# A bidirectional RWKV-7 scan: half of the output norm two slots later, three copies and squares reordered, and the old state added by one whole-array product

## The chip, the cores and the metric

The kernel runs on one core of one Trainium2 chip, as one launch. TensorE (PE, with its weight loads as PEld), VectorE (DVE), ScalarE (ACT), GpSimd (POOL) and SyncE (SP, which here only issues DMAs) each work through their own instruction queue in order. The metric is the device time of one execution in microseconds (us), lower is better. Before the change the median of three runs is 4229.61 us (4223.09 to 4233.41).

## The reference

The kernel computes two encoder layers over 1280 tokens (256 of a prompt, 1024 of a sample) with 1024 channels: a bidirectional RWKV-7 mixer with an MLP, then a neighbourhood attention with an MLP. The change lies in the mixer alone. Cut to that:

```python
def step(S, inp):                       # one token; S is 64 x 64 for each of 16 heads
    r_t, w_t, k_t, v_t, a_t, b_t = inp
    sa = jnp.einsum('bhvk,bhk->bhv', S, a_t)
    S = S * w_t[:, :, None, :] + sa[..., None] * b_t[:, :, None, :] + v_t[..., None] * k_t[:, :, None, :]
    return S, jnp.einsum('bhvk,bhk->bhv', S, r_t)
# run forward (d = 0) and backward (d = 1); y is the sum of both
mu = jnp.mean(y, axis=-1, keepdims=True)
var = jnp.mean(jnp.square(y - mu), axis=-1, keepdims=True)
y = ((y - mu) * lax.rsqrt(var + GN_EPS)).reshape(B, T, C) * lnx_g + lnx_b
y = y + (bonus * vf).reshape(B, T, C)
out = (y.astype(h.dtype) * g) @ w_o
```

## The kernel before

**Jobs and slots.** The recurrence is taken in chunks of 64 tokens. Two heads share the 128 partitions, one in the lower and one in the upper 64. A job is 16 chunks of such pairs; there are ten jobs (two of prompt chunks, eight of sample chunks), and each takes 16 steps, one a slot. In step i the forward direction works on chunk i and the backward one on chunk 15 - i, so that step 15 finishes the last of the job's y. A state starts anew at slot 0 of jobs 2 to 9 and at slots 0, 4, 8 and 12 of jobs 0 and 1.

**The order.** All work of the scan is registered with `at(slot, function)`. The list is sorted by slot time, and each of PE, DVE, ACT and POOL gets its instructions in just that order; no planner moves them. SP's DMAs are issued in the order of the same list. A job's preparation (masks, a triangular inverse by rank-1 updates on DVE, lines 874 to 880, and its transfers) is registered up to 41 slots ahead of the job itself, so that in every slot the engines also do work for later jobs.

**One step** (`scan_step`, k is the step's number over all jobs). It uses two PSUM banks, bx and by, of two each, taken in turn by k: A and sn (the new state) lie in bx, Y and U in by.
- s0 at i - 0.64: PE adds the products of v into sn (`bx<-vv,ll`), Y (`by<-vv,zz`) and A (`bx<-vv,zz`).
- s1 at i: PE adds the old state's products into Y and A (`by<-S,x`, `bx<-S,x`).
- s1c at i + 0.1: ACT copies A to up (line 1040).
- s2 at i + 0.3: PE makes U from up (`by<-up,qq`).
- s2b at i + 0.32: PE adds the old state into sn, by products with the identity (`bx<-S,cst`). It is left out where a state starts or ends.
- s0 of step i + 1 follows at i + 0.36.
- s2c at i + 0.38: ACT copies U to u (line 1060).
- s3 at i + 0.58: PE adds u's products into sn and Y (`bx<-u,ll`, `by<-u,zz`).
- s3c at i + 0.66: ACT scales sn to the new state S (line 1075), in two instructions.
- s4 at i + 0.75: ACT copies Y to y (line 1080), or in steps 8 to 15 to y2 (line 1083), which s5 at i + 0.97 adds to y on DVE (line 1087).

Products of 64x64 name a quadrant of the PE array by the partitions that they read and write. Those of s2, s2b and `bx<-u,ll` read and write the same half (diagonal quadrants); `bx<-vv,ll` and `bx<-vv,zz` read one half and write the other (off-diagonal). Each 32-bit float product is issued as two passes.

**Beside the steps**, for later steps, PE makes kps (line 960, one PSUM buffer), which DVE masks to zz (line 965) at .95 of each slot and ACT copies to ll (line 970) at .74. The products kps of the next slot can't start until both have read it.

**The norm of a job's y** (`scan_post`) is made in two halves of eight chunks: the first takes the middle chunks 4 to 11, the second chunks 0 to 3 and 12 to 15. Each half is a chain registered from t0 on: bonus times v on DVE (p0) and a bias on POOL, mean (p1) and subtraction (p2) on DVE, squares on ACT (p2b, line 1138), their sum on DVE (p2c, line 1142), rsqrt on DVE and ACT (p3, with Ln and Exp, lines 1151 and 1152), scaling on DVE (p4) and POOL, eight transposing products on PE (tr, line 1167, zps), and p5, a copy to zt on ACT (line 1171) with eight DMAs to z_d that POOL issues (line 1176). The squares' tile and zt share one buffer:

```python
st["sq"] = self.yp.tile([P, 8, 64], F32, name="ysq", tag="ysq", bufs=1)
zt = self.yp.tile([P, 4, 2, 64], F32, name="zt", tag="ysq", bufs=1)
```

t0 is 12.9 for the first half and 16.9 for the second, which so falls into slots 1 to 5 of the next job; the second half of the last job has times of its own.

Of the kernel before, what the change touches and what calls it, by code (L numbers as in the profile page):

```python
# [24 lines left out]
HALVES = ((slice(0, 64), slice(64, 128)), (slice(64, 128), slice(0, 64)))  # L25
# [24 lines left out]
class Trunk:  # L50
# [739 lines left out]
    def at(self, t, f, level=3):  # L790
        self.todo.append((t, len(self.todo), f, level))
# [204 lines left out]
    def scan_step(self, at, J, st, grp, k, i, new, end):  # L996
        nc = self.nc
        mm = lambda out, a, b, start, stop: nc.tensor.matmul(out, a, b, start=start, stop=stop, skip_group_check=True)  # L998
        second = i >= 8
        dirs = []  # L1000
        for d, cc in enumerate((i, 15 - i)):
            m, c0 = grp[cc // 4]
            dirs.append((d, cc // 4, cc % 4, cc, m, c0 + cc % 4))
        pair = lambda t: t[:, :P].rearrange("p (d v) -> p d v", d=2)
        R = {}

        def banks():
            x, y = self.b_x[k % 2], self.b_y[k % 2]
            return pair(x), pair(y), pair(x[:, P:2 * P]), pair(y[:, P:2 * P])
        zz = lambda d, g, c, e: J["zz", d, g, c // 2][:, c % 2, e]  # L1010
        ll = lambda d, g, c, e: J["ll", d, g, c // 2][:, c % 2, e]

        def s0():
            A, Y, sn, U = banks()
            v = J["v"]
            for d, g, c, cc, m, ch in dirs:
                for e, (es, eo) in enumerate(HALVES):
                    if not end:
                        mm(sn[es, d], ll(d, g, c, e)[eo], v[eo, cc], d == 0, False)
            for d, g, c, cc, m, ch in dirs:  # L1020
                yd = 1 - d if second else d
                for e, (es, eo) in enumerate(HALVES):
                    mm(Y[eo, yd], zz(d, g, c, e)[eo, 64:128], v[eo, cc], d == 0, False)
                    mm(A[es, d], zz(d, g, c, e)[eo, 0:64], v[eo, cc], end and d == 0, new)

        def s1():
            A, Y, sn, U = banks()
            R["S"] = S = None if new else st["S"]
            if S is None:
                return  # L1030
            for d, g, c, cc, m, ch in dirs:
                yd = 1 - d if second else d
                for es, eo in HALVES:
                    mm(Y[eo, yd], J["x", d, g][es, 3, c], S[es, d], False, False)
                    mm(A[es, d], J["x", d, g][es, 2, c], S[es, d], False, True)

        def s1c():
            A, Y, sn, U = banks()
            R["up"] = self.sp.tile([P, 2, 64], F32, name="up", tag="up", bufs=2)
            nc.scalar.copy(R["up"], A)  # L1040

        def s2():
            A, Y, sn, U = banks()
            for d, g, c, cc, m, ch in dirs:
                for es, eo in HALVES:
                    mm(U[es, d], J["Q"][es, cc, d], R["up"][es, d], False, True)

        def s2b():
            A, Y, sn, U = banks()
            S = R["S"]  # L1050
            if S is None or end:
                return
            for d in range(2):
                for es, eo in HALVES:
                    mm(sn[es, d], self.ident[es, es], S[es, d], False, False)

        def s2c():
            A, Y, sn, U = banks()
            R["u"] = self.sp.tile([P, 2, 64], F32, name="u", tag="u", bufs=2)
            nc.scalar.copy(R["u"], U)  # L1060

        def s3():
            A, Y, sn, U = banks()
            for d, g, c, cc, m, ch in dirs:
                yd = 1 - d if second else d
                for e, (es, eo) in enumerate(HALVES):
                    if not end:
                        mm(sn[es, d], ll(d, g, c, e)[es], R["u"][es, d], False, True)
                    mm(Y[eo, yd], zz(d, g, c, e)[es, 64:128], R["u"][es, d], False, True)

        def s3c():
            A, Y, sn, U = banks()
            S = st["S"] = self.sp.tile([P, 2, 64], F32, name="S", tag="S", bufs=3)
            for d, g, c, cc, m, ch in dirs:
                nc.scalar.activation(S[:, d], sn[:, d], AF.Copy, scale=self.dall[:, m, d, ch:ch + 1])

        def s4():
            A, Y, sn, U = banks()
            if not second:
                nc.scalar.copy(J["y"][:, i:16 - i:15 - 2 * i], Y)  # L1080
            else:
                R["y2"] = self.sp.tile([P, 2, 64], F32, name="y2", tag="y2", bufs=2)
                nc.scalar.copy(R["y2"], Y)

        def s5():
            y = J["y"][:, 15 - i:i + 1:2 * i - 15]
            nc.vector.tensor_tensor(out=y, in0=R["y2"], in1=y, op=ALU.add)
        at(i - 0.64, s0)
        at(i, s1)
        at(i + 0.1, s1c)  # L1090
        at(i + 0.3, s2)
        at(i + 0.32, s2b)
        at(i + 0.38, s2c)
        at(i + 0.58, s3)
        if not end:
            at(i + 0.66, s3c)
        at(i + 0.75, s4)
        if second:
            at(i + 0.97, s5)

    def scan_post(self, at, J, grp, left):

        nc = self.nc
        for half in range(2):
# [64 lines left out]
            def p5(st=st, runs=runs):  # L1169
                zt = self.yp.tile([P, 4, 2, 64], F32, name="zt", tag="ysq", bufs=1)  # L1170
                nc.scalar.copy(zt, st["zps"])
                for x, (m, c0) in enumerate(runs):
                    dst = self.scr["z_d"][m].rearrange("(e v) (c t) -> e v c t", e=2, t=64)
                    for par in range(2):
                        for e in range(2):
                            nc.gpsimd.dma_start(dst[e, :, c0 + par:c0 + 4:2], zt[64 * par:64 * par + 64, 2 * x:2 * x + 2, e])  # L1176
            t0 = (12.9, 16.9)[half]
            if left == 0 and half == 1:
                when = (-2.0, -1.9, -0.1, 0.0, 0.1, 0.2, 0.3, 0.4, 0.5, 0.6, 0.65, 0.7, 0.9)
            else:  # L1180
                when = (0.2, 0.7, 0.6, 0.95, 1.15, 1.45, 1.6, 1.75, 1.95, 2.3, 3.0, 4.36, 4.62)
            for dt, f in zip(when, (p0, lambda f=lnx: f(1), p1, p2, p2b, p2c, lambda f=p3: f(0), lambda f=p3: f(1), lambda f=p3: f(2), p4,
                                    lambda f=lnx: f(0), tr, p5)):
                at(t0 + dt, f)
# [777 lines left out]
```

## Time and profile before

| | |
|---|---|
| median of three runs | 4229.61 us |
| profiled execution | 4222.5 us |
| its span, first to last instruction | 4220.7 us |
| mean granted TensorE clock | 0.942 |
| scan (first to last copy of up) | 760.5 to 1458.7 us |
| PE, DVE, ACT, POOL busy | 91%, 59%, 36%, 31% of the span |
| copies of up, of u | 160 each, 0.28 and 0.27 us |
| squares (line 1138) | 20, 0.63 us each |

All rows come from one profiled execution. In the timeline a row gives its start, its length, engine, line, operation, the names out<-in, shapes, and in brackets how long the engine had been idle and what ended that. In groups the columns are busy time, mean length in ns of one, and the idle time just before, with what ended it. PE's products are pipelined: a row's end is modelled, its start is what to read.

### The profile page before, as it was taken

What the parts mean: (1) busy time and instruction counts of PE and PEld (TensorE: products, weight loads), DVE (VectorE), ACT (ScalarE), POOL (GpSimd) and SP (SyncE); (2) the same over time, 40 slices, a digit from 0 to 9 for tenths busy, and PEclk for the clock granted to TensorE, in tenths of its full rate; (3) what the DMA queues carried; (4) which work ended last, traced back from release to release, by engine and by line L of the source; (5) the groups of instructions that cost most, each with busy time, mean ns of one, the idle gap of its engine ahead of it and who ended that gap; (6) DMA issues with size and microseconds to landing.
All of it is one profiled execution on the core that took longest, in us unless ns stands there. A gap on an engine that the chain in (4) does not pass through costs nothing.

```text
span 4220.7 us, 87911 instructions
## 1 busy us (share of the span) xinstructions
PE 3832.4 (91%) x35700; PEld 3222.3 (76%) x35700; DVE 2505.8 (59%) x4850; ACT 1513.9 (36%) x3651; POOL 1293.3 (31%) x1234
## 2 busy tenths in 40 slices
PE   7897879777777699999999999989989999999999
PEld 4665668677766587888888879867767888888888
DVE  7888973657565347555555563366665755555555
ACT  6776651333444432111111123355554311111111
POOL 5440001132323344222222241244344422222222
PEclk8997879898898899999999999999998999999999
DMA  3326565765654241111111115333334111111111
GB/s 110 87 96 207 196 198 154 195 170 153 159 160 118 83 152 60 41 36 36 41 40 41 35 46 165 100 78 66 76 86 154 61 35 41 41 41 41 35 36 60
DMA packets 385798, 393.55 MB, mean 93 GB/s; under 512 B 161872, under 2 KB 306480, under 8 KB 384112
## 3 DMA queue, kind: packets, MB, share of 16 engines
q1 hardware_dynamic: 331760, 315.42, 26.1%
q10 hardware_dynamic: 46704, 61.35, 4.2%
q0 software_dynamic: 6928, 11.15, 1.0%
q8 instruction: 280, 4.59, 0.5%
q14 instruction: 126, 1.03, 0.1%
HBM read 277.80 MB, written 121.24 MB: 95 GB/s over the span
## 4 chain that ended last, share of the span: by engine, by line
PE 64%; DVE 6%; ACT 3%; DMA 3%; POOL 2%; issue 2%; SPq 0%; ACTq 0%; DVEq 0%; POOLq 0%
PE ps L96 17%; PE ps L98 17%; PE ps L97 17%; PE by L998 2%; PE kps L960 2%; PE bx L998 2%; PE op L1877 1%; POOL z_d L1176 1%; PE pt L1819 1%; PE zps L1167 1%; DVE q L880 1%; PE nst L1614 1%; DMA z_d<-zt 1%; DVE tmp L878 1%; PE s L1801 1%
## 5 line engine op out<-in xcount | busy, mean ns | idle before, releaser
L1434 DVE TENSOR_TENSOR x<-ps,x 128x256 f32<-128x256 f32 x1488 | 814.0, 594 | 629.2 <-PE ps L98 629.1
L96 PE MATMUL ps<-ah,whi 128*128 128x512 f32 (+1 forms) x2304 | 843.5, 366 | 4.6 <-ACT whi L90 4.6
L98 PE MATMUL ps<-ah,wlo 128*128 128x512 f32 (+1 forms) x2304 | 824.2, 358 | 2.7 <-POOL wlo L91 2.5
L97 PE MATMUL ps<-al,whi 128*128 128x512 f32 (+1 forms) x2304 | 823.4, 357 | 0.0
L91 POOL TENSOR_TENSOR wlo<-raw,whi 128x1024 fp32r<-128x1024 f32 (+1 forms) x178 | 390.6, 2195 | 860.4 <-ACT whi L90 826.8
L96 PE MATMUL ps<-hh,whi 128*128 128x512 f32 (+1 forms) x1536 | 548.2, 357 | 11.6 <-DVE x L1434 11.6
L98 PE MATMUL ps<-hh,wlo 128*128 128x512 f32 (+1 forms) x1536 | 546.8, 356 | 0.0
L97 PE MATMUL ps<-hl,whi 128*128 128x512 f32 (+1 forms) x1536 | 546.5, 356 | 0.0
L96 PEld LDWEIGHTS ps<-ah,whi 128*128 128x128 f32 x2304 | 438.6, 190 | 79.1 <-issue 11.9
L98 PEld LDWEIGHTS ps<-ah,wlo 128*128 128x128 f32 x2304 | 437.6, 190 | 69.1 <-POOL wlo L91 3.6
L97 PEld LDWEIGHTS ps<-al,whi 128*128 128x128 f32 x2304 | 438.5, 190 | 60.2 <-issue 1.1
L90 ACT CAST whi<-raw 128x1024 fp32r<-128x1024 f32 (+1 forms) x206 | 200.7, 974 | 705.8 <-PE ps L97 634.4
L96 PEld LDWEIGHTS ps<-hh,whi 128*128 128x128 f32 x1536 | 292.3, 190 | 55.1 <-DVE x L1434 14.1
L1413 POOL TENSOR_TENSOR rl<-rl 128x512 f32<-128x512 f32 (+1 forms) x192 | 174.4, 909 | 500.1 <-PE ps L98 458.3
L98 PEld LDWEIGHTS ps<-hh,wlo 128*128 128x128 f32 x1536 | 292.2, 190 | 41.4
L97 PEld LDWEIGHTS ps<-hl,whi 128*128 128x128 f32 x1536 | 292.3, 190 | 41.1
L1412 ACT ACTIVATE rl<-ps 128x512 f32<-128x512 f32 (+1 forms) x192 | 100.8, 525 | 546.0 <-PE ps L98 546.0
L1415 ACT CAST hh<-rl 128x512 fp32r<-128x512 f32 (+1 forms) x192 | 105.5, 549 | 321.1 <-POOL rl L1413 321.0
L1416 DVE TENSOR_TENSOR hl<-rl,hh 128x512 fp32r<-128x512 f32 (+1 forms) x192 | 119.3, 622 | 151.7 <-ACT hh L1415 151.4
L965 DVE TENSOR_TENSOR zz<-kps,cst 128x512 f32<-128x512 f32 x160 | 110.0, 688 | 159.9 <-ACT ll L970 159.8
L960 PE MATMUL kps<-x 64*64 64x192 f32 x2560 | 171.7, 365 | 18.2 <-DVE zz L965 10.9
L1812 POOL TENSOR_TENSOR s<-s,mx 128x384 f32<-128x384 f32 (+1 forms) x154 | 117.0, 770 | 212.8 <-DVE mx L1811 148.3
(313 smaller groups left out, 7826.1 us busy)
## 6 DMA issues: line engine op xcount, KB each, us to landing
x<-x_d SPq DMA_DIRECT2D x88, 512.0 KB, 4.7
raw<-in_w_down_dram SPq DMA_DIRECT2D x64, 512.0 KB, 3.2
raw<-in_w_up_dram SPq DMA_DIRECT2D x64, 512.0 KB, 3.3
eab<-x_d SPq DMA_DIRECT2D x80, 256.0 KB, 4.6
x_d<-ar ACTq DMA_DIRECT2D x32, 512.0 KB, 3.1
x_d<-bk ACTq DMA_DIRECT2D x32, 512.0 KB, 4.3
bs<-tab SPq DMA_DIRECT2D x128, 96.0 KB, 3.9
v_d<-vt ACTq DMA_DIRECT2D x80, 128.0 KB, 4.0
```

What stands on the lines that cost most here:

```text
L90: nc.scalar.copy(hi[:, cs], raw)
L91: lo_eng.tensor_tensor(out=lo[:, cs], in0=raw, in1=hi[:, cs].bitcast(F32), op=ALU.subtract)
L96: mm(ps, sh, mh, start=first, stop=False)
L97: mm(ps, sh, ml, start=False, stop=False)
L98: mm(ps, sl, mh, start=False, stop=last)
L960: mm(J["kp"][out, e, 192 * c:192 * c + 192], x[es, b, 2 * pr + c], x[es, 2:5, 2 * pr + c], start=True, stop=True)
L965: nc.vector.tensor_tensor(out=z, in0=src[:, :, :, :P], in1=self.mask[d].unsqueeze(1).unsqueeze(1).to_broadcast([P, 2, 2, P]), op=ALU.mult)
L998: mm = lambda out, a, b, start, stop: nc.tensor.matmul(out, a, b, start=start, stop=stop, skip_group_check=True)
L1413: nc.gpsimd.tensor_tensor(out=r[:, :n], in0=r[:, :n], in1=r[:, :n], op=ALU.mult)
L1416: nc.vector.tensor_tensor(out=hl[:, :n], in0=r[:, :n], in1=hh[:, :n].bitcast(F32), op=ALU.subtract)
L1434: nc.vector.tensor_tensor(out=xv, in0=ps[:, :n], in1=xv, op=ALU.add)
L1812: nc.gpsimd.tensor_tensor(out=s[:, :nk], in0=s[:, :nk], in1=mx[:, 2:3].to_broadcast([P, nk]), op=ALU.mult)
```

## The change

Four things change. The four 64x64 products of s2b (two directions by two halves) become one product of the whole 128x128 identity with both directions of the state. The copy of Y (s4) moves from i + 0.75 to i + 1.15, which is behind the next step's copy of up at i + 1.1, and the add of s5 from i + 0.97 to i + 1.2. The second half of a job's norm starts at 18.9 instead of 16.9, except in the last job. In both halves (again except the last job's second) the squares and what follows them move by 0.1 to 0.3 slots: the squares from t0 + 1.15 to t0 + 1.45, their sum from 1.45 to 1.75, the rsqrt steps from 1.6, 1.75, 1.95 to 1.9, 2.05, 2.25, the scaling from 2.3 to 2.5 and POOL's from 3.0 to 3.1. The transposes and z_d stay at t0 + 4.36 and t0 + 4.62.

```diff
@@ scan_step
             S = R["S"]
             if S is None or end:
                 return
-            for d in range(2):
-                for es, eo in HALVES:
-                    mm(sn[es, d], self.ident[es, es], S[es, d], False, False)
+            mm(sn, self.ident, S, False, False)
@@ scan_step
         at(i + 0.58, s3)
         if not end:
             at(i + 0.66, s3c)
-        at(i + 0.75, s4)
+        at(i + 1.15, s4)
         if second:
-            at(i + 0.97, s5)
+            at(i + 1.2, s5)
@@ scan_post
-            t0 = (12.9, 16.9)[half]
+            t0 = (12.9, 18.9 if left else 16.9)[half]
             if left == 0 and half == 1:
                 when = (-2.0, -1.9, -0.1, 0.0, 0.1, 0.2, 0.3, 0.4, 0.5, 0.6, 0.65, 0.7, 0.9)
             else:
-                when = (0.2, 0.7, 0.6, 0.95, 1.15, 1.45, 1.6, 1.75, 1.95, 2.3, 3.0, 4.36, 4.62)
+                when = (0.2, 0.7, 0.6, 0.95, 1.45, 1.75, 1.9, 2.05, 2.25, 2.5, 3.1, 4.36, 4.62)
```

## The prediction

> **What bounds the kernel now.** I read the page's span and chain first, then the groups and waits of the scan (about 760 to 1,465 us), then the timeline around one job boundary. The page:
>
> ```profile
> span 4220.7 us, 87911 instructions
> ...
> PE ps L96 17%; PE ps L98 17%; PE ps L97 17%; PE by L998 2%; PE kps L960 2%; PE bx L998 2%; PE op L1877 1%; POOL z_d L1176 1%; PE pt L1819 1%; PE zps L1167 1%; DVE q L880 1%; PE nst L1614 1%; DMA z_d<-zt 1%; DVE tmp L878 1%; PE s L1801 1%
> ```
>
> Half of the chain is dense products (L96 to L98) that the change doesn't touch. What it can touch is the scan, where the chain has two things that compute nothing: issuing z_d (L1176) and its transfer. The squares' own line (its instructions, then what ACT idled for ahead of them) says who pays for that:
>
> ```profile
> L1138 ACT ACTIVATE ysq<-y x20: 629/630/632, 814.3 to 1466.3; 128x512 f32<-128x512 f32 x20
>   DMA z_d<-zt: 49.4, 8
>   DVE y L1134: 17.1, 11
>   DVE q L880: 5.5, 1
> ```
>
> Twenty squares, two halves for each of ten jobs. Nine of them (8 + 1) stand idle for 49.4 + 5.5 = 54.9 us. Nine is the number of boundaries between jobs: by the schedule the second half's squares run early in the next job, at its slot 2.05. The timeline of one boundary shows why they wait:
>
> ```profile
> 1124.40 0.60 ACT L1171 COPY zt<-zps 128x512 f32<-128x512 f32 x1
> ...
> 1125.29 4.79 POOL L1176 DMA_DIRECT2D z_d<-zt  x8 [7.24 <-ACT S L1075]
> ...
> 1131.87 0.63 ACT L1138 ACTIVATE ysq<-y 128x512 f32<-128x512 f32 x1 [5.31 <-DMA z_d<-zt]
> 1132.41 0.25 ACT L1040 COPY up<-bx 128x128 f32<-128x128 f32 x1
> ```
>
> zt and ysq share one buffer (tag "ysq", bufs 1). The squares wait until zt's eight transfers have left it, and the copy of up, on which the whole scan hangs, is queued behind the squares. Busy time by stage around it (stretch, its length, then PE, PEld, DVE, ACT and POOL busy, granted clock, DMA share, GB/s):
>
> ```profile
> 1103.00:1118.50 15.50, 10.95 (x346) 9.30 (x339) 14.92 (x35) 6.33 (x26) 4.39 (x3) 0.89 0.62 199
> 1118.50:1126.70 8.20, 8.17 (x184) 7.66 (x184) 7.79 (x20) 2.64 (x10) 1.41 (x3) 0.79 0.34 65
> 1126.70:1132.40 5.70, 0.00 (x0) 0.00 (x0) 3.02 (x6) 0.53 (x1) 4.67 (x7) 0.71 0.71 149
> 1132.40:1136.50 4.10, 3.79 (x104) 3.72 (x104) 2.59 (x9) 1.91 (x10) 0.00 (x0) 0.57 0.02 4
> 1136.50:1142.80 6.30, 5.70 (x222) 5.17 (x218) 5.16 (x13) 3.50 (x16) 1.28 (x1) 1.00 0.75 230
> ```
>
> In the third row PE does nothing; in the fourth it runs at a granted clock of 0.57, in the fifth at 1.00. The first two rows show the next limit: DVE is busy 14.92 of 15.5 and 7.79 of 8.2 us.
>
> **The change part by part.**
>
> **A, second half two slots later.** zt of the first half is copied at slot 17.52, the squares move from 18.05 to 20.35, some 2.8 slots behind. The last stage row holds two slots, 3.15 us each; 2.8 of them are 9 us; the transfers took 1131.87 - 1124.40 = 7.5 us. So the wait goes: -54.9 us. So do nine squares between the old-state products and up, 9 x 0.63 = -5.7. Late next are the squares in slot 4, behind their DVE subtraction, and the copy of u is now queued behind them: +0.6 each, +5.4 (0 to 12). The z_d issues (POOL) go from slot 5.5 to 7.5 of the next job; POOL is busy 1.28 of 6.3 us in the last stage row and the gate reads z_d only after the scan, so nothing. The transposes (PE, zps) move by the same two slots at equal cost. If slots shrank below 2.7 us, this cover would be gone and the wait would begin to come back.
>
> **B, the clock.** Behind each stall a slot takes 4.1 us at 0.57; the next two take 3.15 at 1.00. Where PE doesn't stand empty I expect most of that back: 9 x 0.8 = -7 (0 to -9).
>
> **C, old state by one whole-array product.** Now four products of 64x64, two passes each:
>
> ```profile
> L998 PE MATMUL bx<-S,cst 64*64 64x64 f32 x1024 | 56.0, 230 | 1.8 <-issue 1.8
> ```
>
> and, in PE's timeline, beside the only whole-array products of the scan, zps (whose pass takes 0.275):
>
> ```profile
> L1167 PE MATMUL zps<-cst,y x160: 275/275/582, 827.9 to 1480.9; 128*128 128x128 f32 x160
> ```
>
> ```profile
> 1143.18 0.45 PE L923 MATMUL yps<-qx,za 64*64 64x32 f32 x8
> 1143.56 0.49 PE L1167 MATMUL zps<-cst,y 128*128 128x128 f32 x2
> ...
> 1145.23 0.39 PE L1167 MATMUL zps<-cst,bv 128*128 128x128 f32 x2
> 1145.55 0.45 PE L998 MATMUL by<-up,qq 64*64 64x64 f32 x8
> 1145.83 0.23 PE L998 MATMUL bx<-S,cst 64*64 64x64 f32 x2
> 1145.84 0.27 PE L998 MATMUL bx<-vv,ll 64*64 64x64 f32 x2
> 1145.89 0.28 PE L998 MATMUL bx<-S,cst 64*64 64x64 f32 x3
> 1145.95 0.22 PE L998 MATMUL bx<-vv,ll 64*64 64x64 f32 x1
> ...
> 1146.41 0.27 PE L998 MATMUL bx<-u,ll 64*64 64x64 f32 x1
> ```
>
> 1024 / 8 = 128 places. A 64x64 pass takes 0.22 and a quadrant starts the next 0.06 later (1145.83, 1145.89). The four quadrants of the array work side by side: bx<-vv,ll of the next slot (off-diagonal quadrants) starts at 1145.84 beside S,cst (diagonal), 0.06 us behind the last up,qq (1145.55 + 0.45 - 0.22 = 1145.78). So S,cst costs the others nothing today. A whole-array product stops them all. Beside zps: the last yps starts at 1143.63 - 0.22 = 1143.41, the first zps 0.15 later, its second pass at 1143.56 + 0.49 - 0.275 = 1143.78, 0.21 later (0.11 when running); the last zps starts at 1145.23 + 0.39 - 0.275 = 1145.34 and the next quadrant product 0.21 behind. So vv,ll would start 0.15 + 0.21 + 0.21 = 0.57 behind up,qq instead of 0.06: +0.50 us on the off-diagonal quadrants. The state needs the diagonal ones: today the products of u start at 1146.41, 0.86 behind the first up,qq, right when u is there and the queue is empty, with no slack. With vv,ll at 0.23 + 0.57 = 0.80, eight pairs of 0.06 behind it, the off-diagonal quadrants are taken until 1.28, and the products of u, which alternate between the two kinds, end 0.3 to 0.4 later than today, those of the state a little before. I take 0.31: 128 x 0.31 = +40 us; ends 128 x 0.2 = 26 (some slots hidden by DVE) and 128 x 0.50 = 64. The Trainium skill, "TensorE: Matmul & The Clock Gate", Part 3, The mechanism, says that matmuls start strictly in program order; by that rule vv,ll waits for all S,cst today (0.23), the change adds only 0.57 - 0.29, some 0.2 less a place, and the time would be about 4172. The rows disagree: vv,ll at 1145.84 starts ahead of S,cst at 1145.89, which the program has first.
>
> **D, Y copied behind up.** Today Y stands in front of up:
>
> ```profile
> 1142.34 0.37 ACT L970 COPY ll<-kps 128x256 f32<-128x256 f32 x1 [0.16 <-PE kps L960]
> 1142.60 0.27 ACT L1080 COPY y<-by 128x128 f32<-128x128 f32 x1
> 1142.76 0.28 ACT L1040 COPY up<-bx 128x128 f32<-128x128 f32 x1
> ```
>
> ```profile
> 1137.37 0.27 ACT L1060 COPY u<-by 128x128 f32<-128x128 f32 x1 [0.55 <-PE by L998]
> ```
>
> ```profile
> L1040 ACT COPY up<-bx x160: 247/279/284, 760.5 to 1458.7; 128x128 f32<-128x128 f32 x160
> ...
>   PE bx L998: 15.9, 48
> ```
>
> Y holds up by 1142.76 - 1142.60 = 0.16 us where ACT, not PE, is late. The last line (ACT's idle time ahead of the 160 up copies) says that 48 waited for PE; so up to 112 x 0.16 = 18, and at least nothing. In its new place Y lies in the 0.55 us that ACT waits for U. Half: -9. Y's bank is written again by the slot after next, 0.8 us behind up: no wait. The add on DVE (now i + 1.2) follows Y; nothing waits for it before the mean.
>
> **E, first half.** Its squares move from ahead of up(14) (14.05) to 14.35, still 0.03 ahead of the copy of u(14) at 14.38, not behind it; Ln and Exp move from ahead of S(14) to ahead of up(15). They wait today 17.1 us (row above; the last job's second half is in it) and
>
> ```profile
>   DVE rqx L1149: 14.7, 9
> ```
>
> ```profile
> L960 PE MATMUL kps<-x 64*64 64x192 f32 x2544 | 169.8, 364 | 18.2 <-DVE zz L965 10.9 <-issue 7.3
> ```
>
> 14.7 us (the idle time ahead of Ln). Little comes free: DVE has no gap in these slots and kps already waits 10.9 us for its masks. -6 (0 to -20).
>
> **DVE's limit.** In the 39.8 us of the five stage rows DVE is busy 33.5 (14.92 + 7.79 + 3.02 + 2.59 + 5.16): at most 6.3 us a boundary, 57 for nine, can go before DVE is full. My terms inside these slots (A 55.2, B 7, E 6, some D 5, less C 17) make 56, at that limit; +4 for the friction.
>
> **Sum:** -60.6 + 5.4 - 7 + 40 - 9 - 6 + 4 = -33 us. The profiled execution took 4222.5 (span 4220.7 and 1.8 around it), 7.1 below the median of 4229.6: 4189.5 for such an execution, 4197 as a median.
>
> **The rivals.**
>
> **R1, slower: the array's switch costs far more than beside zps.** Place: up,qq to products of u, 128 times. Without C the sum is -73, so 0.57 us a place makes no change and from 0.67 (+86) it is slower by 0.3%. At 0.7 it is +90 - 73: 4246. For: zps' first pass follows half-length products (64x32), up,qq's are 64x64, and where the granted clock is low every step of the switch is longer. Against: 0.50 is the whole price by the rows, and PE's chain sees part of it. The Trainium skill, "TensorEngine Tiling (Array Packing)", Key Properties, says that a change of tiling mode drains the engine; the 0.15 and 0.21 above agree, and no run here shows it between these products.
>
> **R2, DVE takes over at the boundary.** DVE's second-half work (about 4 us) now meets the rank-1 updates in slots 3 to 5, masks come late, PE waits at kps. Then of the 56 us inside the boundary slots half is lost to waiting, and with C and D outside them (+23 and -4) -28 + 19 = -9 is left: 4221, no difference. For: 14.92 of 15.5. Against: 2.59 of 4.1 and 5.16 of 6.3 where the work goes.
>
> **R3, C is hidden.** If u's copy, not PE's queue, sets the products of u (u late by Y and squares), C costs 128 x 0.1 = 13: 4170. The skill's rule of program order above lands beside it (4172); against the rows I give it 0.02 of this rival's chance.
>
> **R4, it doesn't do what it says:** squares in front of u at both halves wait some 2 us for DVE, 19 x 2 = 38 us, instead of 5.4: 4230, same.
>
> **How the numbers follow.** Forecast (4180 to 4214) 0.50, R3 0.17, R2 0.12, R4 0.06, R1 0.15. About 0.3% (12.7 us) is what a measurement tells from no change. Faster: 0.50 + 0.17 + a third of R2 = 0.71; same: the rest of R2 and R4 = 0.14; slower: R1 = 0.15. The range runs from R3 with more of D and E (4162) to just over no change (4234), leaving out most of R1.
>
> **What would show it.** A: no DMA wait at the squares. B: 1.00 clock in slots 2 and 3. C: 256 products 128*128 from S, vv,ll 0.57 behind up,qq's last, products of u 1.0 or more behind its first. D: more than 48 up copies waiting for PE. E: Ln no longer ahead of S(14). Wrong would make it: products of u over 1.4 behind up,qq (R1), PE waiting over 40 us for zz at kps (R2), long waits of u's squares (R4).

## The result, and the profile after

The changed kernel takes 4181.85 us (median of four, 4178.03 to 4185.51) where the kernel before takes 4227.39 (median of four, 4223.09 to 4233.41). The ratio is 0.9891, with a 95% interval of 0.9874 to 0.9908: 46 us less, between 39 and 53. The forecast was 4197, 33 less.

The page of the kernel after (line numbers behind 1050 are smaller by 2):

```profile
span 4182.7 us, 86363 instructions
...
PE 3851.5 (92%) x34932; PEld 3226.1 (77%) x34932; DVE 2493.6 (60%) x4850; ACT 1520.2 (36%) x3651; POOL 1292.8 (31%) x1234
...
PE ps L96 17%; PE ps L98 17%; PE ps L97 17%; PE bx L998 3%; PE by L998 2%; PE kps L960 2%; DVE q L880 1%; PE op L1875 1%; PE pt L1817 1%; PE zps L1165 1%; DVE tmp L878 1%; PE nst L1612 1%; DMA bs<-tab 1%; PE s L1799 1%; PE vps L512 1%
```

The two entries that computed nothing, z_d's issue and its transfer, are no longer among the chain's costliest. The squares' line of the kernel after shows the same (its instructions, then ACT's idle time in front of them, us and times):

```profile
L1136 ACT ACTIVATE ysq<-y x20: 629/630/631, 819.5 to 1437.1; 128x512 f32<-128x512 f32 x20
...
  DVE y L1132: 14.5, 12
  DVE q L880: 3.5, 1
```

No DMA is named in it (49.4 us before); the 14.5 us are a wait for DVE's subtraction. The 3.5 us are not what their label says. They lie at one boundary, and the chain of the kernel after (start, length, what) still runs through z_d there:

```profile
1321.25 0.65 POOL z_d L1174
1321.90 2.36 issue
1324.26 2.97 POOL z_d L1174 x6
...
1327.75 5.28 DMA z_d<-zt
...
1333.14 0.04 ACT ysq L1136
```

POOL stood still for 2.36 us behind its first z_d transfer, so the last one landed at 1333.03, 12.7 us behind zt's copy (1320.35), and the squares started 0.1 us later, though the subtraction that feeds them had ended at 1331.5. So the wait for the buffer is gone at eight of the nine boundaries and shorter at the ninth (3.5 us, 7.7 before). The timeline of ACT over the boundary that the prediction shows, kernel after (start, length, then what was idle before):

```profile
1116.03 0.60 ACT L1169 COPY zt<-zps 128x512 f32<-128x512 f32 x1
1118.74 0.27 ACT L1040 COPY up<-bx 128x128 f32<-128x128 f32 x1 [0.38 <-PE bx L998]
...
1125.77 0.27 ACT L1040 COPY up<-bx 128x128 f32<-128x128 f32 x1 [0.38 <-PE bx L998]
1126.39 0.63 ACT L1136 ACTIVATE ysq<-y 128x512 f32<-128x512 f32 x1 [0.19 <-DVE y L1132]
1126.93 0.25 ACT L1058 COPY u<-by 128x128 f32<-128x128 f32 x1
```

zt is copied at 1116.03, in slot 1, and the squares follow at 1126.39, in slot 4: 10.4 us apart, more than the 7.8 that the transfers took here (7.5 before). ACT waits 0.19 us there, where it waited 5.31. The squares do stand ahead of the copy of u, as the prediction noted from the slot numbers.

Next, engines by stage, one row for the whole scan (first to last copy of up) of each kernel: stretch, length, busy PE, PEld, DVE, ACT, POOL, granted clock, DMA share, GB/s. Before:

```profile
760.50:1458.70 698.20, 535.21 (x16920) 484.49 (x16920) 426.30 (x1015) 288.19 (x1161) 205.27 (x290) 0.89 0.56 147
```

After:

```profile
764.20:1429.60 665.40, 572.19 (x16152) 501.53 (x16152) 415.43 (x1012) 294.51 (x1160) 205.20 (x291) 0.92 0.59 153
```

These two rows hold most of the result. The scan is 32.8 us shorter, though PE is busy 37.0 us longer: its idle time went from 163.0 to 93.2 us. (The profiled execution after took 4184.5, 38 less than the one before; the other 5 us lie outside the scan, where profiles of all these kernels scatter by a few us. In a second profile of the same changed kernel the scan took 651.9, so one profile's scan is known to some 14 us.) What PE waited for between 755 and 1465 us, which in the kernel after reaches past the end of the scan (line and releaser, us, times and longest), before:

```profile
PE by L998 <- ACT up L1040: 103.1, 85, 9.1
PE kps L960 <- DVE zz L965: 10.9, 10, 2.6
PE bx L998 <- issue: 9.6, 9, 2.8
PE by L998 <- issue: 8.7, 9, 2.4
PE kps L960 <- issue: 6.9, 6, 2.7
PE qps L935 <- issue: 5.9, 4, 1.8
```

After:

```profile
PE by L998 <- ACT up L1040: 38.8, 92, 1.8
PE kps L960 <- DVE zz L965: 16.7, 13, 3.2
...
PE bx L998 <- ACT u L1058: 11.7, 12, 3.0
PE by L998 <- issue: 8.3, 11, 2.2
...
PE kps L960 <- issue: 4.6, 4, 1.7
PE qps L935 <- issue: 4.2, 4, 1.4
```

The wait for up lost 64 us and its longest case fell from 9.1 to 1.8. Small new waits came, for u (11.7) and more for the masks zz (+5.8, of which 3.5 inside the scan). The last wait to look at is called "issue": PE waits for nothing that the profile names. It, too, shrank, and this turns out to matter.

The clock at the boundary, by stage in the kernel after (slot 1, slot 2, slots 3 and 4 from 1121.9):

```profile
1112.90:1118.70 5.80, 5.72 (x142) 5.19 (x138) 4.13 (x11) 2.27 (x9) 1.78 (x3) 1.00 0.11 15
1118.70:1121.90 3.20, 2.84 (x95) 2.54 (x96) 2.96 (x9) 1.78 (x8) 3.00 (x6) 1.00 0.66 177
1121.90:1129.40 7.50, 6.95 (x222) 6.10 (x218) 7.22 (x19) 4.30 (x17) 1.27 (x1) 1.00 0.98 253
```

Slot 2 runs at 1.00 where it ran at 0.57. The price of the whole-array product stands in PE's timeline of the kernel after:

```profile
1142.52 0.45 PE L998 MATMUL by<-up,qq 64*64 64x64 f32 x8 [0.44 <-ACT up L1040]
1142.90 0.49 PE L998 MATMUL bx<-S,cst 128*128 128x128 f32 x2
1143.32 0.27 PE L998 MATMUL bx<-vv,ll 64*64 64x64 f32 x2
...
1143.73 0.27 PE L998 MATMUL bx<-u,ll 64*64 64x64 f32 x2
```

The last up,qq starts at 1142.52 + 0.45 - 0.22 = 1142.75, the first pass of S,cst 0.15 behind it, its second at 1142.90 + 0.49 - 0.275 = 1143.115, 0.21 later, and vv,ll 0.205 behind that: 0.57 in all, to the hundredth the price read beside zps. Over the 122 such places at full clock the medians of the three steps are the same. The products of u start 1.21 behind the first up,qq, where it was 0.86.

The table gives mean distances between neighbouring copies of up, us, worked out from ACT's timeline of each run (six jobs, 2 to 7). Slot 1 is the way from the copy in slot 1 to that in slot 2, and so on. The last row is the median of slot 6, where little else is in the way; it stands for an undisturbed slot. A second profile of the changed kernel has 67.0 for the whole job, 19.5 for slots 0 to 4 and 14.6 for 13 to 15, so differences of this size between columns can be scatter.

| slots | before | half_later | whole_array | chain_spread | own_buffer | after | after_four |
|---|---|---|---|---|---|---|---|
| 1 | 11.64 | 5.40 | 12.09 | 5.40 | 7.00 | 5.96 | 5.48 |
| 2 | 4.12 | 2.81 | 4.95 | 9.13 | 5.68 | 3.17 | 2.81 |
| 3 | 3.65 | 5.40 | 4.01 | 4.12 | 4.61 | 3.90 | 3.62 |
| 0 to 4 | 25.98 | 20.60 | 28.39 | 24.39 | 23.71 | 20.11 | 18.99 |
| 13 to 15 | 13.88 | 14.31 | 13.81 | 15.29 | 14.13 | 14.91 | 15.03 |
| whole job | 72.8 | 68.0 | 73.9 | 72.8 | 70.8 | 68.9 | 66.9 |
| slot 6, median | 2.80 | 2.75 | 3.20 | 2.80 | 2.80 | 3.12 | 2.68 |

### The profile page after: what moved, and what is told of

It reads as the page before. It is cut to its first block, busy times and chain, and to the rows that moved or that the text cites. A ratio compares the mean times of both kernels' runs of the same rounds, so it can differ in the third digit from the quotient of the medians.

```text
span 4182.7 us, 86363 instructions
## 1 busy us (share of the span) xinstructions
PE 3851.5 (92%) x34932; PEld 3226.1 (77%) x34932; DVE 2493.6 (60%) x4850; ACT 1520.2 (36%) x3651; POOL 1292.8 (31%) x1234
## 4 chain that ended last, share of the span: by engine, by line
PE 65%; DVE 7%; ACT 2%; DMA 2%; issue 2%; POOL 2%; SPq 1%; ACTq 0%; DVEq 0%; POOLq 0%
PE ps L96 17%; PE ps L98 17%; PE ps L97 17%; PE bx L998 3%; PE by L998 2%; PE kps L960 2%; DVE q L880 1%; PE op L1875 1%; PE pt L1817 1%; PE zps L1165 1%; DVE tmp L878 1%; PE nst L1612 1%; DMA bs<-tab 1%; PE s L1799 1%; PE vps L512 1%
## 5 line engine op out<-in xcount | busy, mean ns | idle before, releaser
L960 PE MATMUL kps<-x 64*64 64x192 f32 x2560 | 171.4, 361 | 21.8 <-DVE zz L965 16.7
```

What stands on the lines that cost most here:

```text
L960: mm(J["kp"][out, e, 192 * c:192 * c + 192], x[es, b, 2 * pr + c], x[es, 2:5, 2 * pr + c], start=True, stop=True)
```

## Experiments: each part alone

Four kernels take one part each, on one chip. The kernel before took 4223.07 there. Here and below the time is a median, while the microseconds more or less follow from the ratio of all runs; the medians' difference can be some 5 us off them.

**Second half two slots later, nothing else.**

```diff
-            t0 = (12.9, 16.9)[half]
+            t0 = (12.9, 18.9 if left else 16.9)[half]
```

> Only t0 of the second half moves, 16.9 to 18.9 (not in the last job). Theory (the wait at the shared buffer was the loss): the 54.9 us of idle ACT and most of the slots at low clock go, the squares stay in front of up: -50 us, and no DMA wait at the squares. Rival (DVE sets the end at the boundary, so the stall comes back as waits for zz): about half, -28 us, with over 40 us of PE waiting for zz at kps.

Measured: 0.9901 (0.9876 to 0.9925), 4176.1 us, 42 less. In the table slot 1 loses 6.24 and slot 2 loses 1.31, but slot 3 gets 1.75 longer. The squares' idle time and, further on, ACT's timeline in this kernel say why:

```profile
  DVE y L1134: 29.3, 19
  DMA z_d<-zt: 5.8, 1
```

```profile
1114.78 0.63 ACT L1138 ACTIVATE ysq<-y 128x512 f32<-128x512 f32 x1 [0.92 <-DVE y L1134]
1115.31 0.25 ACT L1040 COPY up<-bx 128x128 f32<-128x128 f32 x1
```

With the old spacing the squares stand in front of the copy of up in slot 4 and wait for DVE's subtraction there: 29.3 us over all the squares, 17.1 before. The later spacing, which puts them behind that copy, is thus part of the stall's cure. Against the expectation one boundary, the same as in the kernel after, keeps a wait for the transfer (5.8 us).

**The whole-array product, nothing else.**

```diff
-            for d in range(2):
-                for es, eo in HALVES:
-                    mm(sn[es, d], self.ident[es, es], S[es, d], False, False)
+            mm(sn, self.ident, S, False, False)
```

> Only s2b becomes one product of the whole array. Theory (entering and leaving the quadrants costs 0.57 us, of which 0.31 reach the step): 128 x 0.31 = +40 us, and slots of 2.80 us become 3.1. Rival 1 (u's copy hides it): +13 us. Rival 2 (the price falls on every step in full): 128 x 0.50 = +64 us.

Measured: 1.0043 (1.0028 to 1.0058), 4240.8 us, 18 more (12 to 24). Busy time over its scan, and PE's issue waits in it:

```profile
764.10:1480.80 716.70, 569.62 (x16152) 499.81 (x16152) 427.78 (x1014) 290.25 (x1161) 205.85 (x291) 0.91 0.54 142
```

```profile
PE kps L960 <- issue: 3.5, 4, 1.1
...
PE by L998 <- issue: 3.0, 4, 1.2
PE bx L998 <- issue: 2.7, 4, 1.1
PE yps L923 <- issue: 2.4, 3, 1.4
...
PE qps L935 <- issue: 1.7, 2, 1.1
```

PE is busy 34.4 us longer, 0.27 a place, but the scan is only 18.5 longer. Undisturbed slots grew by 0.40 (2.80 to 3.20), which over 128 places would be 51. What came back stands in the second fence: these issue waits sum to 13.3 us, those of the kernel before to 37.4 (the four rows above, and smaller ones). That is 24 less. PE's waits for up grew by 7 meanwhile, so its idle time fell by 16 in all, the difference between 34.4 and 18.5. The gain lies where the issue waits were: slot 9 went from 6.41 to 4.31 and slot 11 from 5.01 to 4.21.

**Y behind up, nothing else.**

```diff
-        at(i + 0.75, s4)
+        at(i + 1.15, s4)
...
-            at(i + 0.97, s5)
+            at(i + 1.2, s5)
```

> Only Y's copy and its add move (i + 0.75 to i + 1.15, i + 0.97 to i + 1.2). Theory: up starts up to 0.16 us earlier where ACT was late: -9 us (-18 to 0). Rival (s1's products end last anyway): within 4 us of no change.

Measured: 0.9995 (0.9981 to 1.0008), 4217.5 us: between 8 less and 3 more, no change that can be told. The mechanism did work. ACT's idle time in front of the copies of up, now waiting for PE:

```profile
  PE bx L998: 28.3, 57
```

57 copies wait for PE, 28.3 us, against 48 and 15.9 before; undisturbed slots shrank by 0.06. ACT got ready earlier and PE did not.

**The later spacing in both halves, nothing else.**

```diff
-                when = (0.2, 0.7, 0.6, 0.95, 1.15, 1.45, 1.6, 1.75, 1.95, 2.3, 3.0, 4.36, 4.62)
+                when = (0.2, 0.7, 0.6, 0.95, 1.45, 1.75, 1.9, 2.05, 2.25, 2.5, 3.1, 4.36, 4.62)
```

> Only the list of times inside a half changes (squares t0 + 1.15 to t0 + 1.45 and what follows); the second half stays at 16.9. The wait at the shared buffer then stands in front of u instead of up and begins 0.3 slots later: theory -6 us from the first halves and some -0.5 us a boundary, -10 in all. Rival (DVE has no gap in slots 13 to 15, and Ln and Exp now stand in front of up): 0 to +10 us, with slot 14 longer by what slot 13 gains.

Measured: 0.998 (0.997 to 0.9989), 4212.7 us, 8 less. The wait for zt is whole (squares' idle time), but it now holds up u (PE's waits):

```profile
  DMA z_d<-zt: 50.7, 9
```

```profile
PE bx L998 <- ACT u L1060: 55.3, 18, 7.0
```

At the boundary slots 0 to 4 got shorter (25.98 to 24.39); where the first half moved, slots 13 to 15, the job got longer, 13.88 to 15.29. In jobs 2 to 7 the two cancel (72.8 both), and in these two profiles the shorter scan comes from the last two jobs (7 us). The four parts alone sum to -42 + 18 - 2 - 8 = -34; together they gave -46. The errors of the five figures together are larger than these 12 us, so the sums don't show that the parts depend on each other. The table does: slot 3 takes 5.40 us in half_later and 3.90 and 3.62 in after and after_four, where the squares stand behind up.

## Experiments: what the stall was made of

**Only the shared buffer taken away.** The kernel before, with zt in another buffer:

```diff
-            zt = self.yp.tile([P, 4, 2, 64], F32, name="zt", tag="ysq", bufs=1)
+            zt = self.yp.tile([P, 4, 2, 64], F32, name="zt", tag="bv", bufs=2)
```

> The kernel before, every time unchanged, but zt takes the buffer ring of bv (tag bv) and no longer that of the squares. Theory (the shared buffer is the whole cause of the stall): no DMA wait at the squares, -45 to -60 us, at least as much as half_later's -42, because the squares' input is ready when up is. Rival (DVE's rank-1 work sets the end of the boundary slots): -28 us or less, PE waiting for zz instead.

Measured: 0.9947 (0.9933 to 0.9961), 4197.7 us, 22 less. The squares no longer wait for a DMA but for DVE (first fence), and PE has a new wait, for S (second fence):

```profile
  DVE y L1134: 25.1, 16
```

```profile
PE by L998 <- ACT S L1075: 19.4, 15, 2.8
```

Without the transfer in the way the same chain at the same place is late by DVE: the rsqrt steps wait for it in front of S (ACT's idle time ahead of Ln is 37.8 us, 14.7 before), and slots 1 to 3 take 17.3 us where the moved chain takes 13.6 (half_later). The DMA alone was so worth about half of what the place was worth. The rival was right on the size, but named the masks where S waited.

**Squares truly behind u.** The kernel after, with the squares at t0 + 1.50 instead of 1.45, behind the copy of u:

```diff
-                when = (0.2, 0.7, 0.6, 0.95, 1.45, 1.75, 1.9, 2.05, 2.25, 2.5, 3.1, 4.36, 4.62)
+                when = (0.2, 0.7, 0.6, 0.95, 1.5, 1.75, 1.9, 2.05, 2.25, 2.5, 3.1, 4.36, 4.62)
```

> The changed kernel with the squares at t0 + 1.50, which is really behind the copy of u (0.38), instead of t0 + 1.45. Theory (u late behind squares that wait for DVE: PE idles 12.5 us for u): -8 to -12 us against the changed kernel. Rival (DVE has no gap there, PE waits for zz instead): within 4 us, with the 12.5 us gone to zz or up.

Measured: 0.991 (0.9894 to 0.9925), 4182.3 us, the same as after. The squares' idle time and PE's wait for masks:

```profile
  DVE y L1132: 8.2, 6
```

```profile
PE kps L960 <- DVE zz L965: 25.6, 12, 5.1
```

PE's wait for u fell from 12.5 to 1.3 us in the scan, the squares' from 14.5 to 8.2, and the wait for masks rose by most of it (in this row, which reaches past the scan, 16.7 to 25.6; inside the scans 13.4 to 20.5). DVE's work is the bound there; whom its lateness meets can be chosen, the lateness stays.

## Experiments: the price of the old state

**The kernel after with the four products of before.**

```diff
-            mm(sn, self.ident, S, False, False)
+            for d in range(2):
+                for es, eo in HALVES:
+                    mm(sn[es, d], self.ident[es, es], S[es, d], False, False)
```

> The changed kernel with s2b as it was (four quadrant products). whole_array alone cost 18 us although its 2.80 us slots became 3.20 (0.40 x 128 = 51), and PE's idle time that waits for nothing shown (issue) fell from 37.4 to 13.3 us. Theory (the whole-array product pays 0.4 a step and gets part of it back because PE needs its instructions later and fewer of them): slots of 3.12 go back to 2.74, issue idle rises from 23.1 to 35 to 40, and the kernel takes 7 to 20 us less than the changed one, about 4168. Rival (in the changed kernel DVE or u hide the product): within 5 us of the changed one.

Measured: 0.9866 (0.9851 to 0.9881), 4163.3 us, 56 less than before. The whole-array product so costs the changed kernel 11 us (0.9891 less 0.9866; the intervals overlap a little), 15 by the second comparison of it (after_again, below). Undisturbed slots shrink from 3.12 to 2.68 and issue waits rise from 23.1 to 41.6 us: the exchange that whole_array showed, the other way round.

**Two products instead of four, each in one quadrant.** Both directions in one product of 128 columns:

```diff
-            mm(sn, self.ident, S, False, False)
+            for es, eo in HALVES:
+                mm(sn[es], self.ident[es, es], S[es], False, False)
```

> The changed kernel with s2b as two quadrant products of 64x64 by 128 columns, one a half: half of the instructions of the four, the same array time, no switch out of the quadrants. Theory (the issue idle comes from the number of PE instructions): slots of 2.74, issue idle under that of after_four by a quarter, 4 to 12 us faster than after_four. Rival (issue idle depends on the pace alone): as after_four, within 4 us.

Measured: 0.9852 (0.9836 to 0.9868), 4158.0 us, 62 less. The products are fewer and the array's division stays. Against the four it is 5 us less, which the overlapping intervals don't tell from nothing. Issue waits are 33.2 us, 8 less than with the four, where the theory had 10.

**The whole-array product and four products of zeros.** The kernel before, with the new product and, beside it, the four small ones with a tile of zeros as data (they add nothing). It has the switch, and more instructions than before; PE's count no longer falls:

```diff
+        self.zero = self.cp.tile([P, 64], F32, name="zero")
+        nc.gpsimd.memset(self.zero, 0.0)
...
+            mm(sn, self.ident, S, False, False)
             for d in range(2):
                 for es, eo in HALVES:
-                    mm(sn[es, d], self.ident[es, es], S[es, d], False, False)
+                    mm(sn[es, d], self.ident[es, es], self.zero[es], False, False)
```

> The kernel before with s2b as one whole-array product and, behind it, four quadrant products of the identity with zeros, so that PE issues more instructions than before instead of fewer. whole_array had 13.3 us of issue idle on PE in the scan, the kernel before 37.4. Theory P (issue idle fell because steps are longer): still 10 to 20 us, and about whole_array's time, +18 us, a little more for the products. Theory N (it fell because there are fewer instructions): 35 us or more, and +35 to +45 us.

Measured: 1.0062 (1.0047 to 1.0077), 4246.1 us, 26 more. Issue waits sum to 21.4 us, between the 13.3 of the whole-array product alone and the 37.4 of before. So 16 of the 24 us of their fall come with the slower pace. The rest may belong to the smaller number of instructions, but two profiles of the changed kernel differ by 4 us in this sum (23.1 and 19.4).

What an issue wait is shows in the kernel before. PE's timeline has such a gap, and the transfers from 1020.5 to 1022.3 have one packet of an instruction queue in them:

```profile
1023.31 0.79 PE L832 MATMUL aps<-eab 64*64 64x64 f32 x9 [1.36 <-issue]
```

```profile
q8 instruction: 1, 0.02, 3.2%
```

All 27 issue gaps over 0.4 us in that scan (and the 14 to 31 of four other kernels) ended 1.2 to 1.8 us after a 16 KB packet of that queue had landed. In that scan 134 such packets landed, one for about 253 of the instructions of PE and PEld, so a moment picked at random lies in such a stretch in about one case of nine. So PE runs out of instructions in dense stretches of small products, and a step that takes longer on the array leaves the fetch more time. No run changed the fetch itself; the cause is as far shown as this coincidence and the zeros' run go. The Trainium skill, "Runtime: NRT & Kernel Launch", Instruction fetch mechanics, holds the fetch to be hidden by the rate at which instructions are issued; the 37.4 us disagree with that for these products.

## Experiments: the best version

Three kernels on one chip; before took 4221.54 there. The changed kernel again:

> The changed kernel once more, as the reference of the next two on the same chip: 0.989 of the kernel before, -38 to -53 us.

Measured: 0.9902 (0.9886 to 0.9917), 4177.9 us. With the two wide products and the squares at t0 + 1.50:

> The changed kernel with s2b as two quadrant products of 128 columns and the squares at t0 + 1.50, behind the copy of u. Theory (the whole array's switch is the part of the change that loses): -15 to -25 us against the changed kernel, nearly all from s2b. Rival (squares behind u matter too): -30 or more.

Measured: 0.9854 (0.9839 to 0.9869), 4158.1 us: 62 less than before and 20 less than the change on the same chip, with intervals apart. The wide products make this difference, since after_two_wide, without the later squares, stands at 0.9852. The same again with the first half's spacing as before the change:

```diff
-                when = (0.2, 0.7, 0.6, 0.95, 1.5, 1.75, 1.9, 2.05, 2.25, 2.5, 3.1, 4.36, 4.62)
+                when = ((0.2, 0.7, 0.6, 0.95, 1.15, 1.45, 1.6, 1.75, 1.95, 2.3, 3.0, 4.36, 4.62) if half == 0 else (0.2, 0.7, 0.6, 0.95, 1.5, 1.75, 1.9, 2.05, 2.25, 2.5, 3.1, 4.36, 4.62))
```

> As after_two_behind, but the first half keeps its old list of times (squares at t0 + 1.15, in front of up). Slots 13 to 15 took 13.9 us a job before and 14.9 in the changed kernel (jobs 2 to 7). Theory (the first half's new times lose about 1 us a job, since DVE is full there and Ln and Exp stand in front of up): -5 to -12 us against after_two_behind. Rival (those slots are DVE's in any order): within 4 us of it.

Measured: 0.9871 (0.9853 to 0.9889), 4163.2 us: 5 to 7 more than its sister (medians, ratios), not told from nothing. Slots 13 to 15 take 13.54 instead of 14.82, as I had expected, but slots 0 to 4 take 20.65 instead of 19.17. This fits DVE doing early in the next job what it doesn't do late in one; no run shows it apart. My theory that undoing this part would gain was wrong.

## Why the prediction was right, and where its numbers were off

**A, the stall: right in mechanism, sharper in the parts.** The squares' wait for the transfers is gone at eight of nine boundaries; the forecast had all nine and took 7.5 us for transfers that can take 12.7. Slot 1 got 6.24 us shorter in half_later, times nine 56; the terms had 60.6. The loss in front of the moved squares was taken as 5.4 (0 to 12); PE's waits for u came to 12.5 us in the scan, 1.4 before, about twice that. With the old spacing it would have been more: slot 3 got 1.75 longer, some 16 us over nine boundaries.

**B, the clock: too small.** Taken as 0.8 us a boundary; slot 2 went from 4.12 to 2.81 in half_later, 1.31, some 12 us. The granted clock is 1.00 in slot 2 at all six boundaries of jobs 2 to 7; before it was 0.50 to 0.59.

**C, the whole-array product: the step that failed, by its size.** The switch (0.57), the 256 products and the late products of u came as read, and PE's busy time rose by 0.27 a place, beside the 0.31 taken. In undisturbed slots the price was even higher, 0.40. But +40 us was the sum on PE's own account and took PE's other waits as fixed. Measured were 18 alone, 11 to 15 inside the change, both below my lower end of 26: 24 us of issue waits disappeared beneath it. The 13 us of R3 were close, by another cause than R3's: not a late u covers the price, but, as far as the packets and the zeros' run show it, instructions that come late anyway. (Products in different quadrants did start out of program order, vv,ll at 1145.84 ahead of S,cst at 1145.89 in the prediction's rows, so what stands ahead of the prediction about queues worked through in order doesn't hold for the starts of PE's products.)

**D, Y behind up: nothing measurable instead of -9.** In the kernel after, ACT's idle time in front of the copies of up is

```profile
  PE bx L998: 34.1, 66
```

so that 66 copies wait for PE, more than the 48, as listed. Half of the 0.16 us was credited to the path. It became idle time of ACT: PE is the one that is late.

**E, first half: its place was wrong.** I looked for -6 from earlier Ln and Exp at slots 13 to 15; these got 1.0 longer a job (13.88 to 14.91). Undone in the best version it costs 5 to 7 us, which the intervals don't tell from nothing, and that at slots 0 to 4. The product isn't the reason, since after_four has 15.03 there. The squares ahead of u wait for DVE, which is R4's mechanism, but for some 16 us in all and not for 38.

**The sum.** Without C the terms gave -73; after_four measured -56 (-63 to -50). Without D and E they are -58. So A, B and the friction agree with it together, 15 us of D and E weren't there, C cost some 25 to 29 less, and the two errors left the forecast 15 us too high. That they run against each other is luck: C alone sized right would have put the forecast near 4170. R1 fell with the 0.57. R2 fell as a whole, PE's waits for masks reached 16.7 us and not 40, but its DVE is where the gain of the later squares went. Program order, the rule of the Trainium skill weighed under C, would have made C cost 0.31 - 0.2 = 0.11 a place, some 14 us in all. The 18 and 11 to 15 measured are near that, but undisturbed slots grew by 0.40 and not by 0.11, so it came out right by the issue waits and not by the rule.

## What to carry to other kernels

When a step is priced on the busiest engine, ask which of that engine's other waits run at the same time, instruction fetch included: a slower step can be paid for partly by waits that it covers, and a faster step can uncover them. A stall at a shared buffer has two prices, the buffer's and the place's: a buffer of its own was worth 22 us here, another place in the order 42. And before small products are joined into one of the whole array, try joining them inside their quadrants: two wide products were 20 us better than one whole.

## What was unexpected of the hardware

PE lost its full clock without one long wait. In the kernel after it fell at 1101.25 us, in a slot 14. The 3.4 us ahead of the fall and the 3.4 behind it (length, busy times, clock as above):

```profile
1097.85:1101.25 3.40, 1.98 (x64) 1.52 (x59) 3.23 (x9) 1.56 (x6) 0.00 (x0) 1.00 0.07 23
1101.25:1104.65 3.40, 2.16 (x48) 1.69 (x42) 3.26 (x10) 0.84 (x3) 0.00 (x0) 0.50 0.42 94
```

PE was busy 1.98 us of the first stretch, and its longest wait there was 0.98 us (for u); a wait of 1.24 us for zz came behind the fall. The Trainium skill, "TensorE: Matmul & The Clock Gate", Part 1, speaks in its table of one idle window of about 3.4 us, and further down of a clock that falls by frequent short idles between groups of products; these rows agree with the second. Slot 14 runs below full clock in most jobs, before as after (0.59 to 0.75 in jobs 2 to 7), and after the change mostly slot 15 too (0.50 to 0.59). DVE is busy 3.23 of 3.40 us in the first row, so a slot that DVE overfills seems to be paid for twice. The other surprise is the instruction fetch above, 37.4 us of the scan before.
